# Transposes moved from TensorE to the DMA for the scan's gated outputs and the first feed-forward's products, with 48 adaLN pieces put off until the scan

## The chip, the cores and the metric

The kernel runs on one core of one Trainium2 chip. The metric is the device time in microseconds of one execution; of several runs the median counts. TensorE is called PE here, its weight load PEld, VectorE DVE, ScalarE ACT, GpSimd POOL and SyncE SP. SP does no arithmetic in this kernel: it issues the loads.

## The reference, cut to what matters

Two transformer layers over 256 tokens of width 2048, all in fp32. Layer 0 mixes by differential attention, layer 1 by a Mamba-2 scan; each is followed by a SwiGLU feed-forward. Both are modulated by a vector `c` (adaLN).

```python
c_act = silu(c)
for i in range(2):
    ada = c_act @ ada_w[i] + ada_b[i]                 # 2048 x 12288 weights a layer
    shift1, scale1, gate1, shift2, scale2, gate2 = split(ada, 6)
    h = rms_norm(x, norm1_g[i]) * (1 + scale1) + shift1
    m = diff_attention(h, ...) if i == 0 else mamba2_ssd(h, ...)
    x = x + gate1 * m
    h = rms_norm(x, norm2_g[i]) * (1 + scale2) + shift2
    g, u = split(h @ w_gate_up[i], 2)
    x = x + gate2 * ((silu(g) * u) @ w_down[i])

# mamba2_ssd, the part after the scan; 8 groups of 512 columns
y = y + d_skip * xs
y = y * silu(z)
y = rms_norm(y by group, norm_g)
return y @ w_out
```

Two places matter. `silu(g) * u` and the normalised `y` come out with tokens on the partitions, and the next matrix product needs them with features on the partitions: both are transposed in between.

## The kernel before, in words

**Tiles and units.** Every large weight is read in units of 256 rows by 512 columns (512 KB), each by one DMA on SP's queue into one of 7 `raw` buffers. `split_unit` makes two fp32r tiles of it: ACT casts `raw` to `wh` (line 287), DVE subtracts it to `wl`. PE then runs the three products wh*h, wl*h and wh*l of the two activation halves `ah` and `al`: 12 matmuls of 512 columns for a unit of 256 rows and all 256 tokens. `wh` and `wl` have 4 buffers each, so ACT and DVE work up to four units ahead of PE. Nearly all instructions are recorded under line 136, that of a metering helper, so the groups are told apart by tile names.

**Order.** The order on every engine is the order in which the program issues. `push_unit` puts the products of a unit into a queue `fifo`; `pop` runs them and then calls `tick`, which does the small work: it starts an adaLN piece when the accumulated `ada["rate"]` reaches one, uses the pieces loaded a tick earlier (`ripe`), and advances every active generator by one `yield` (`step_all`). A step of a generator is thus one unit of PE work.

**adaLN pieces.** The vectors of both layers are summed on DVE from 512 KB pieces of `ada_w`, which take `raw` buffers and SP's queue like the weights. `col_jobs` makes 32 pieces for one vector, used by `col_sum`: a multiply with a broadcast copy of `silu(c)` (`cB`, two tiles) and a sum along the row, on DVE, shown as CUSTOM_DVE_ANT_0. `ada_job` makes 34 pieces for a gate vector, used by a multiply-add into `acc`, and at each half POOL reduces `acc` over the partitions. In the first feed-forward 128 column pieces are queued (`m1` and `f1`, two vectors each) at a rate of 128/164 a unit; in the scan the 34 of gate `m1` at 34/140 (`ADA_UNITS`).

**First feed-forward (`ffn(0)`).** Eleven blocks `j`, each of 8 gate units and 8 up units. `up_done` multiplies silu(gate) by up into `sg` (DVE). A generator then makes `aT_j`: in layer 0 `rest`, with 8 PE transposes into `wk` banks and two ACT copies; in layer 1 `by_dma`, in which ACT writes the upper and lower 16-bit halves of `sg` apart into `halves`, the ACT queue issues a DMA transpose of 16-bit elements into `aT_j`, and `words` puts the halves together again (ACT) just before the split for the product with `w_down`.

**Scan.** Eight groups `g`, each of 8 units of `x` columns and 8 of `z` columns. `x_steps` is the convolution of a group, `y_steps` the scan and gating. At its end y is scaled by the norm (`r`), transposed by 4 PE transposes for each token block `b`, and DVE multiplies the result by the norm's gain into `yT`. `split(cp, g)` makes `ah` and `al` of it for the product with `ssd_w_out`; this begins at the last `z` block.

## Time and profile before

| | us |
|---|---|
| median of 3 runs | 2661.1 (2660.35 to 2661.39) |
| the profiled execution's own time | 2660.28 |
| its span in the trace | 2658.6 |
| first feed-forward, gate and up | 524 to 1005 |
| first feed-forward, down | 1010 to 1206 |
| scan, 8 groups | 1370 to 1741 |
| product with `ssd_w_out` | 1741 to 1920 |
| second feed-forward, gate and up | 1946 to 2424 |

The stage borders are read from the chain of waits and are rounded. Of an execution 1.7 us lie outside the span, and the profiled execution was 0.8 us faster than the median. In the rows `xN` is a count, "mean ns of one" includes what lies under the next instruction of the same engine, and "idle before" is idle time just before a group with what ended it.

### The profile page before, as it was taken

Reading aid. Unit: us, or ns where it says so; the run is one execution under the profiler, and the core shown is the slowest. Engines: PE = TensorE matmul, PEld = TensorE weight load, DVE = VectorE, ACT = ScalarE, POOL = GpSimd, SP = SyncE. Lnnn points to the kernel's source line nnn. Section 1 sums busy time; section 2 is a strip of 40 time slices with the busy share of each in tenths; the row PEclk is TensorE's granted clock in tenths of the full one; section 3 lists DMA queues with packets and bytes.
Section 4 is the critical chain, followed back from the end, with each engine's and each line's share of the span. In section 5 each row is a group of like instructions: output and inputs, shape, how many; then the busy total and the mean of one; then the engine's idle time right before and its main releaser. Section 6 shows DMA issues by size and latency. Waiting matters only on the chain.

```text
span 2658.6 us, 36556 instructions
## 1 busy us (share of the span) xinstructions
PE 2613.0 (98%) x13625; PEld 2186.6 (82%) x13625; DVE 1883.4 (71%) x2335; ACT 1361.5 (51%) x1897; POOL 200.7 (8%) x282
## 2 busy tenths in 40 slices
PE   7999999999999999999999999999999999999999
PEld 5777777788888888888999989988888888888887
DVE  3779887887788776777777787786654444446776
ACT  5445664644444444446546556565564444445554
POOL 5004331000000000001000010001000000000101
PEclk9999999999999999999999999999999999999999
DMA  9997888699999987885466566666756767677775
GB/s 335 336 350 282 328 297 323 228 343 330 341 341 339 333 320 260 284 291 176 168 229 227 207 245 224 207 225 201 223 158 206 208 203 208 204 207 235 292 282 188
DMA packets 211591, 690.34 MB, mean 260 GB/s; under 512 B 44962, under 2 KB 45299, under 8 KB 210003
## 3 DMA queue, kind: packets, MB, share of 16 engines
q1 hardware_dynamic: 186016, 678.59, 72.3%
q10 hardware_dynamic: 23954, 5.97, 2.2%
q0 software_dynamic: 1440, 3.44, 0.5%
q8 instruction: 107, 1.75, 0.3%
q14 instruction: 74, 0.60, 0.1%
HBM read 679.97 MB, written 2.16 MB: 257 GB/s over the span
## 4 chain that ended last, share of the span: by engine, by line
PE 88%; DVE 4%; DMA 3%; issue 2%; ACT 2%; POOL 0%; ACTq 0%; SPq 0%; DVEq 0%; POOLq 0%
PE mm L136 72%; PE wk L136 12%; PE po L136 4%; DVE wl L136 2%; DMA raw<-in_da_w_in 2%; DVE raw L136 1%; ACT wh L287 1%; DMA raw<-in_ada_m 1%; DMA piece<-in_ada_m 0%; DVE x L136 0%; DVE res L136 0%; ACT x L1042 0%; DMA stage<-in_ada_b 0%; DMA raw<-in_ssd_w_in 0%; DVE mx L136 0%
## 5 line engine op out<-in xcount | busy, mean ns | idle before, releaser
L287 ACT CAST wh<-raw 128x1024 fp32r<-128x1024 f32 (+1 forms) x888 | 925.7, 1046 | 1122.9 <-PE mm L136 715.1
L136 DVE TENSOR_TENSOR wl<-raw,wh 128x1024 fp32r<-128x1024 f32 (+1 forms) x888 | 1085.8, 1232 | 506.2 <-ACT wh L287 502.0
L136 PE MATMUL mm<-wh,ah 128*128 128x512 f32 (+1 forms) x2560 | 1012.8, 396 | 5.8 <-ACT wh L287 3.3
L136 PE MATMUL mm<-wl,ah 128*128 128x512 f32 (+1 forms) x2560 | 997.9, 390 | 1.0 <-DVE wl L136 1.0
L136 PE MATMUL mm<-wh,al 128*128 128x512 f32 (+1 forms) x2560 | 998.2, 390 | 0.0
L136 PEld LDWEIGHTS mm<-wh,ah 128*128 128x128 f32 x2560 | 481.6, 188 | 115.4 <-issue 12.1
L136 PEld LDWEIGHTS mm<-wh,al 128*128 128x128 f32 x2560 | 481.4, 188 | 101.8 <-DVE al L136 0.5
L136 PEld LDWEIGHTS mm<-wl,ah 128*128 128x128 f32 x2560 | 481.9, 188 | 99.5 <-DVE wl L136 2.8
L136 DVE CUSTOM_DVE_ANT_0 raw<-raw,cB,half 128x1024 f32<-128x1024 f32 x110 | 140.8, 1280 | 0.5
L136 DVE CUSTOM_DVE_ANT_0 raw<-raw,cB,bias 128x1024 f32<-128x1024 f32 x110 | 140.7, 1279 | 0.0
L136 PE MATMUL wk<-wh,ah 128*128 128x512 f32 x360 | 140.1, 389 | 0.0
L136 PE MATMUL wk<-wl,ah 128*128 128x512 f32 x360 | 140.1, 389 | 0.0
L136 PE MATMUL wk<-wh,al 128*128 128x512 f32 x360 | 140.1, 389 | 0.0
L531 POOL PARTITION_ALL_REDUCE gate<-acc x12 | 42.5, 3586 | 1273.9 <-DVE acc L136 1267.3
L136 PE MATMUL mm<-ah,wh 128*128 128x256 f32 x720 | 118.8, 285 | 0.0
L136 PE MATMUL mm<-ah,wl 128*128 128x256 f32 x720 | 117.7, 283 | 0.0
L136 PE MATMUL mm<-al,wh 128*128 128x256 f32 x720 | 117.7, 283 | 0.0
L136 DVE SCALAR_TENSOR_TENSOR acc<-raw,cT,acc 128x1024 f32<-128x1024 f32 x90 | 115.0, 1277 | 0.0
L136 PEld LDWEIGHTS mm<-ah,wh 128*128 128x128 f32 x720 | 100.2, 192 | 0.1
L136 PEld LDWEIGHTS mm<-ah,wl 128*128 128x128 f32 x720 | 100.2, 192 | 0.0
L136 PEld LDWEIGHTS mm<-al,wh 128*128 128x128 f32 x720 | 100.2, 192 | 0.0
L136 PEld LDWEIGHTS wk<-wh,al 128*128 128x128 f32 x360 | 67.6, 188 | 14.0
(317 smaller groups left out, 2095.7 us busy)
## 6 DMA issues: line engine op xcount, KB each, us to landing
raw<-in_ffn_w_gate_up SPq DMA_DIRECT2D x352, 512.0 KB, 4.7
raw<-in_ada_t SPq DMA_DIRECT2D x220, 512.0 KB, 5.4
raw<-in_ffn_w_down SPq DMA_DIRECT2D x176, 512.0 KB, 5.3
raw<-in_ssd_w_in SPq DMA_DIRECT2D x136, 512.0 KB, 4.6
raw<-in_da_w_in SPq DMA_DIRECT2D x96, 512.0 KB, 5.9
raw<-in_ada_w SPq DMA_DIRECT2D x96, 512.0 KB, 5.4
raw<-in_ssd_w_out SPq DMA_DIRECT2D x64, 512.0 KB, 4.5
raw<-in_ada_m SPq DMA_DIRECT2D x60, 512.0 KB, 6.0
```

The source lines that it names most:

```text
L136: return fn(dst, *a, **k)
L287: act.copy(wh[:, :, :n], raw)
L531: pool.partition_all_reduce(mods["G", key][:, o:o + 512], acc[:, i * 512:(i + 1) * 512], 128, ReduceOp.add)
```

## The change

In the first feed-forward `rest` goes and `by_dma` is used in both layers, with `words` after it: 88 PE transposes and 22 ACT copies go, 22 ACT copies to `halves`, 22 DMA transposes and 22 ACT copies to `word` come. In the scan the same is done for groups 0 to 6 with a tile `halves` of its own (group 7 keeps the PE transposes and uses that tile for its result): 56 PE transposes go. The two word copies wait `LANDING` steps (6, and 4 more for the second) after the second DMA transpose is issued, and DVE multiplies by the gain from `word` back into the planes. `split` first finishes the group's generator.

Of the 64 pieces of `f1` 16 stay in the first feed-forward (80 pieces there, so the rate is 80/164); 48 are put off to the scan, ahead of the 34 of the gate, at a rate of 82/156. Since `cB` shares its buffers with `acc`, `silu(c)` is kept in DRAM (`cd`, two DMAs of 4 KB) and read back as two broadcasts of 512 KB on SP when the scan stage is entered.

```diff
@@ -33,7 +33,8 @@
 RIPE = 1
 PACE = 4
 EPI = 3
-ADA_UNITS = 140
+ADA_UNITS = 156
+F1_EARLY = 16
 
 
 PIECES = {
@@ -47,6 +48,7 @@
 GRANULES = [(0, 256), (256, 256), (512, 512), (1024, 512), (1536, 512)]
 COLUMN_GRANULES = (1, 2, 3, 4)
 LAG = 2
+LANDING = 6
 
 
 class Laid:
@@ -1372,22 +1374,11 @@
                     yield
                 aT.append(t)
 
-            def rest():
-                yield
-                t = st["top" if j < 6 else "low"].tile([128, 4, 256], F32, name=f"aT_{j}")
-                for b in range(2):
-                    ps = bank("wk")
-                    for i in range(4):
-                        pe.transpose(ps[:, i * 128:(i + 1) * 128], sg[b][:, i * 128:(i + 1) * 128], ident)
-                    act.copy(t[:, :, b * 128:(b + 1) * 128], ps.rearrange("p (k t) -> p k t", k=4))
-                aT.append(t)
-            active.append(by_dma() if layer else rest())
+            active.append(by_dma())
 
         hl = {}
 
         def words(j, a):
-            if layer == 0:
-                return aT[j][:, 2 * a:2 * a + 2, :]
             w = st["low"].tile([128, 512], F32, tag="word", name="word", bufs=2)
             act.copy(w.bitcast(U16).rearrange("p (k t h) -> p h k t", k=2, h=2),
                      aT[j].rearrange("p (h k) t -> p h k t", h=2)[:, :, 2 * a:2 * a + 2, :])
@@ -1473,11 +1464,19 @@
         act.activation(H["aneg"], H["aneg"], AF.Exp)
         dve.tensor_scalar(H["aneg"], H["aneg"], -1.0, None, op0=ALU.mult)
 
+    later = deque()
+    cd = tc.dram_tile([1, 2048], F32, name="cd")
+
     def jobs0():
         col_jobs(1, 0, "m1")
         col_jobs(1, 1, "m1", n1c[1])
+        n = len(jobs)
         col_jobs(1, 3, "f1")
         col_jobs(1, 4, "f1", n2c[1])
+        while len(jobs) > n + F1_EARLY:
+            later.appendleft(jobs.pop())
+        for i in range(2):
+            sp.dma_start(cd[0:1, i * 1024:(i + 1) * 1024], cB[i][0:1, :])
 
     end = ffn(0, end, jobs0, False)
     if upto == "ffn0":
@@ -1489,6 +1488,13 @@
     S = {}
     norm = Norm(0, mods["S", "m1"], mods["T", "m1"])
     acd = tc.dram_tile([64, 256], F32, name="acd")
+
+    def later_jobs():
+        for i in range(2):
+            cB[i] = rowp.tile([128, 1024], F32, tag="acc", name="cB", bufs=2)
+            sp.dma_start(cB[i], bass.AP(tensor=cd.tensor, offset=cd.offset + i * 1024, ap=[[0, 128], [1, 1024]]))
+        jobs.extend(later)
+        later.clear()
 
     def enter():
         end["leave"]()
@@ -1508,6 +1514,7 @@
         pool.affine_select(out=tri, in_=tri, pattern=[[1, 128]], compare_op=ALU.is_ge, fill=0.0,
                            base=0, channel_multiplier=-1)
         S["bc"] = bp.tile([128, 16, 256], F32, name="bc")
+        later_jobs()
         ada_job(1, 2, fin_gate("m1"), gate=True)
         ada.update(rate=0.0)
 
@@ -1624,6 +1631,7 @@
         yield
         phb.close()
         S["y1"] = ph.enter_context(tc.tile_pool(name="y1", bufs=1))
+        S["halves"] = S["y1"].tile([128, 2, 512], F32, name="halves")
         S["gq"] = phq.enter_context(tc.tile_pool(name="gq", bufs=1, side="right"))
         load_decay(0)
         yield
@@ -1658,6 +1666,9 @@
         sp.dma_start(abc, bass.AP(tensor=acd.tensor, offset=acd.offset + 8 * g * 256,
                                   ap=[[0, 128], [256, 8], [1, 256]]))
 
+    def words(planes, b):
+        return planes[:, b].rearrange("p a t -> p (a t)").bitcast(F32).rearrange("p (k t) -> p k t", k=4)
+
     def y_steps(g, banks):
         h0 = 8 * g
         while ("abc", g) not in S:
@@ -1729,7 +1740,30 @@
         dve.tensor_scalar(y[0], y[0], r[0], None, op0=ALU.mult)
         yield
         r.append(rstd_of(ss[1], 1, 512, "yr"))
-        yT = S["yT", g] = S["y0" if g < 4 else "y1"].tile([128, 2, 4, 128], F32, name=f"yT{g}")
+        yp = S["y0" if g < 4 else "y1"]
+        if g < 7:
+            planes = S["yT", g] = yp.tile([128, 2, 8, 128], U16, name=f"yT{g}")
+            for b in range(2):
+                halves = S["halves"][:, b, :].bitcast(U16)
+                act.copy(halves.rearrange("p (h n) -> p h n", h=2),
+                         y[b].bitcast(U16).rearrange("p (n h) -> p h n", h=2))
+                if b:
+                    S["done", g] = True
+                yield
+                act.dma_start_transpose(planes[:, b], halves)
+                if b == 0:
+                    dve.tensor_scalar(y[1], y[1], r[1], None, op0=ALU.mult)
+                    yield
+            for b in range(2):
+                for _ in range(LANDING - 2 * b):
+                    yield
+                w = tmp("word")
+                act.copy(w.bitcast(U16).rearrange("p (k t h) -> p h k t", k=4, h=2),
+                         planes[:, b].rearrange("p (h k) t -> p h k t", h=2))
+                dve.tensor_tensor(words(planes, b), w.rearrange("p (k t) -> p k t", k=4),
+                                  H["cb"][:, 48 + 4 * g:52 + 4 * g, None].to_broadcast([128, 4, 128]), op=ALU.mult)
+            return
+        yT = S["yT", g] = S["halves"].rearrange("p b (k t) -> p b k t", k=4)
         for b in range(2):
             yield from take("wk")
             ps = bank("wk")
@@ -1776,7 +1810,9 @@
     def split(cp, g):
         if g == 7 and cp == 0:
             flush_steps()
-        hl[cp, g] = split_act([(lambda t, b=b: t[:, :, b * 128:(b + 1) * 128], S["yT", g][:, b]) for b in range(2)])
+        step_until(yg[g])
+        hl[cp, g] = split_act([(lambda t, b=b: t[:, :, b * 128:(b + 1) * 128],
+                                S["yT", g][:, b] if g == 7 else words(S["yT", g], b)) for b in range(2)])
 
     call(lambda: ada.update(rate=len(jobs) / ADA_UNITS))
     for g in range(8):
```

On PE, at the border between two blocks of the first feed-forward, before (`sg` is the product to be transposed, `ident` the identity; `mm` and `wk` are banks in PSUM):

```order
L136 MATMUL mm<-wl,ah 128x512
L136 MATMUL mm<-wh,al 128x512
L136 MATMUL wk<-ident,sg 128x128 x8
L136 MATMUL mm<-wh,ah 128x512
L136 MATMUL mm<-wl,ah 128x512
```

The row in the middle is gone after the change; the products on both sides follow each other. On ACT at the first such border, after the change (before, two copies of line 1382 from `wk` to `aT` stood here, and nothing else between the casts):

```order
L1358 ACTIVATE sg<-mm 128x512 x2
L289 CAST wh<-raw 128x1024 x9
L1370 COPY halves<-sg 128x1024
L289 CAST wh<-raw 128x1024
L1373 DMA_TRANSPOSE aT_5468<-halves 128x8x128
L289 CAST wh<-raw 128x1024
L1370 COPY halves<-sg 128x1024
L289 CAST wh<-raw 128x1024
L1373 DMA_TRANSPOSE aT_5468<-halves 128x8x128
L289 CAST wh<-raw 128x1024 x4
```

The two halves of the tokens go one after the other, one unit's cast between each step.

On DVE in the scan, in the first units of a `z` block, where the convolution of one group (`xc`) and the gating of the group before it (`xsd`) meet, before:

```order
L136 TENSOR_TENSOR xe<-xdt,toend 128x512
L136 TENSOR_TENSOR wl<-raw,wh 128x1024
L136 SCALAR_TENSOR_TENSOR xc<-mm,cw_5121,xc 128x253
L136 SCALAR_TENSOR_TENSOR xc<-mm,cw_5121,xc 128x254
L136 SCALAR_TENSOR_TENSOR xc<-mm,cw_5122,xc 128x255
L136 TENSOR_TENSOR xsd<-wk,xsd 128x512
L136 SCALAR_TENSOR_TENSOR xc<-mm,cw_5121,xc 128x253
L136 SCALAR_TENSOR_TENSOR xc<-mm,cw_5121,xc 128x254
L136 SCALAR_TENSOR_TENSOR xc<-mm,cw_5122,xc 128x255
L136 TENSOR_TENSOR wl<-raw,wh 128x1024
```

And after, from the third convolution tile of a group on (the ISA rows are `col_sum`; the short one reads out its sum):

```order
L138 SCALAR_TENSOR_TENSOR xc<-mm,cw_5125,xc 128x255
L138 TENSOR_TENSOR wl<-raw,wh 128x1024
L138 ISA raw,col4f_5139<-raw,cB,half 128x1024
L138 ISA col4f_5139 128x1
L138 TENSOR_TENSOR yT_13928<-word,cb 128x512
L138 TENSOR_TENSOR yi<-po,eac_10811 128x512
L138 TENSOR_TENSOR xsd<-xsd,yi 128x512
L138 SCALAR_TENSOR_TENSOR xc<-mm,cw_5124,xc 128x253
L138 SCALAR_TENSOR_TENSOR xc<-mm,cw_5124,xc 128x254
L138 SCALAR_TENSOR_TENSOR xc<-mm,cw_5125,xc 128x255
L138 TENSOR_TENSOR wl<-raw,wh 128x1024
```

A piece and the gain multiply of the group before (`yT<-word`) now stand between two subtractions of `wl` there.

## The prediction

> **What bounds the kernel now.** I read the page's first part, then the stages by windows, then the chain of waits in order of time, then the groups and timelines of the stages that the change touches.
>
> ```profile
> PE 2613.0 (98%) x13625; PEld 2186.6 (82%) x13625; DVE 1883.4 (71%) x2335; ACT 1361.5 (51%) x1897; POOL 200.7 (8%) x282
> ...
> core 0: us, PE busy (x) PEld busy (x) DVE busy (x) ACT busy (x) POOL busy (x), PEclk, DMA share, GB/s
> 524.00:1005.00 481.00, 481.00 (x2169) 399.30 (x2169) 382.21 (x467) 211.02 (x230) 2.16 (x4) 1.00 0.92 331
> 1369.75:1741.20 371.45, 371.09 (x2420) 336.38 (x2419) 291.31 (x357) 224.98 (x339) 21.17 (x28) 1.00 0.66 233
> 1946.00:2424.00 478.00, 478.00 (x2110) 395.92 (x2109) 232.07 (x210) 226.38 (x236) 0.00 (x0) 1.00 0.69 204
> ...
> 1485.10:1536.32 51.22, 51.22 (x339) 46.61 (x339) 40.22 (x49) 31.11 (x48) 2.24 (x5) 1.00 0.65 228
> ```
>
> PE is busy for the whole of both feed-forward stages and for all but 0.36 us of the scan; the last row is one group of the scan, which repeats every 51.22 us. A busy PE need not be a PE at its peak, so I look at what it runs. The chain in order of time (start, us, what):
>
> ```profile
> 782.87 43.54 PE mm L136 x192
> 827.28 43.54 PE mm L136 x192
> ...
> 1945.87 478.75 PE mm L136 x2112
> ```
>
> A block of the first feed-forward is 192 matmuls in 43.54 us, 0.2268 us each, and the next begins 44.41 us after it. The second feed-forward, whose transposes go by DMA already, runs 2112 matmuls in one piece at 478.75/2112 = 0.2267 us. So PE streams at the same pace in both, no wait is hidden in it, and what stands between two blocks (0.87 us) is the 8 transposes. The profile contains a full-length example of the changed feed-forward.
>
> **PE transposes removed: -15.7 us.** First feed-forward: 11 borders of 44.41 - 43.54 = 0.87 us, 9.6 us. Scan, PE's timeline around four of them:
>
> ```profile
> 1487.48 0.39 PE L136 MATMUL mm<-wh,al 128*128 128x512 f32 x1
> 1487.71 0.60 PE L136 MATMUL wk<-ident,xsd 128*128 128x128 f32 x4
> 1488.06 0.48 PE L136 MATMUL mm<-wh,ah 128*128 128x512 f32 x1
> 1488.38 0.39 PE L136 MATMUL mm<-wl,ah 128*128 128x512 f32 x1
> ```
>
> From the transposes' start to the next product's is 0.35 us, and that product takes 0.32 us to the one behind it in place of 0.23: 0.44 us for four. Two such sets for each of 7 groups make 6.2 us. As PE is the chain there, all 15.7 us come off unless something else falls behind. The rest of the sum is what that could be.
>
> **The added work and its prices**, by groups, DMA queues of three windows (540 to 980, 1390 to 1740 and 1960 to 2390 us) and one tile's landing times:
>
> ```profile
> L136 DVE CUSTOM_DVE_ANT_0 raw<-raw,cB,bias 128x1024 f32<-128x1024 f32 x110 | 140.7, 1279 | 0.0
> L136 DVE DVE_READ_ACCUMULATOR2_ANT half<- 128x1 f32 x110 | 8.9, 81 | 0.0
> L136 DVE SCALAR_TENSOR_TENSOR acc<-raw,cT,acc 128x1024 f32<-128x1024 f32 x90 | 115.0, 1277 | 0.0
> L1368 ACT COPY halves<-sg 128x1024 uint16<-128x1024 uint16 x22 | 22.9, 1043 | 0.0
> L1392 ACT COPY word<-aT 128x1024 uint16<-128x1024 uint16 x22 | 28.1, 1342 | 0.0
> ...
> q1 hardware_dynamic: 40703, 148.22, 93.0%
> ...
> q1 hardware_dynamic: 20665, 78.93, 64.2%
> ...
> q10 hardware_dynamic: 21120, 5.25, 12.2%
> ...
> aT<-halves ACTq DMA_TRANSPOSE x20, 5.5
> ...
> DMA to landing us min/median/max: 3.0/5.5/8.3
> ```
>
> A column piece costs DVE 1.28 + 0.08 = 1.36 us, a gate piece 1.28. A 512 KB load takes 0.930 x 440 us x 512 KB/148.22 MB = 1.45 us of all 16 DMA engines, a DMA transpose 0.122 x 430/20 = 2.62 us.
>
> First feed-forward. DVE loses 48 pieces, 65 us. ACT gains 22 x 1.04 us in a stage where it is busy 211 of 481; the 22 word copies come in the down product, where the second feed-forward has them too. DMA for a block: before 16 units and 16 x 128/164 = 12.5 pieces, 28.5 x 1.45 = 41.3 of 44.41 us (93%); after 16 + 7.8 loads and two transposes, 34.5 + 5.2 = 39.7 of 43.54 us (91%). No fuller than now, only burstier: 0 us. The cover is the seven raw buffers and the four units split ahead; without it the two transposes of a border would cost their 5.2 us.
>
> Scan, for a group (16 units). DVE: 40.22 us now, of which 16 x 34/140 = 3.9 gate pieces are 5.0; after, 16 x 82/156 = 8.4 column pieces are 11.4: 46.6 us of 51.22 - 0.87 = 50.35, or 93%. The gain multiply has the same size as now. ACT: 31.11 + 2 x (1.04 + 1.34) = 35.9 us, and two DMA issues. DMA: 0.642 x 51.22 + 4.5 x 1.45 + 2 x 2.62 = 44.6 us (89%). So DVE is the tightest, and its queue is in order; the units ahead of PE decide. Its idle time in that group, and the place where it is fullest:
>
> ```profile
> L136 DVE TENSOR_TENSOR wl<-raw,wh 128x1024 fp32r<-128x1024 f32 x16 | 19.4, 1218 | 3.9 <-ACT wh L287 3.9
> L136 DVE SCALAR_TENSOR_TENSOR xc<-mm,cw,xc 128x253 f32<-128x253 f32 (+2 forms) x12 | 5.8, 481 | 2.4 <-ACT xc L1520 2.0
> L136 DVE TENSOR_TENSOR abc<-abc,cb 128x1024 f32<-128x1024 f32 x2 | 2.4, 1220 | 1.1 <-ACT abc L1688 1.1
> L136 DVE TENSOR_TENSOR yT<-wk,cb 128x512 f32<-128x512 f32 x2 | 1.4, 688 | 1.3 <-PE wk L136 1.3
> L136 DVE TENSOR_TENSOR xsd<-wk,dsk 128x512 f32<-128x512 f32 x2 | 1.4, 685 | 1.9 <-PE wk L136 1.9
> ...
> 1526.15 1.22 DVE L136 TENSOR_TENSOR wl<-raw,wh 128x1024 fp32r<-128x1024 f32 x1
> 1530.48 1.21 DVE L136 TENSOR_TENSOR wl<-raw,wh 128x1024 fp32r<-128x1024 f32 x1
> ...
> 1536.08 0.48 PE L136 MATMUL mm<-wh,ah 128*128 128x512 f32 x1
> ```
>
> The cast for the unit that PE starts at 1536.08 follows the release of its buffer, so its `wl` is the one at 1530.48, done at 1531.7: 4.4 us early. After the change two pieces and a gain multiply come in front of it since DVE last stood caught up: 2 x 1.28 + 0.69 = 3.2 us, so about 1.2 us of lead is left. It should hold in most groups; where three pieces fall into the burst, PE waits some tenths. Lower bound 0; upper bound in the second rival. Near the lower one, since all waits but that for ACT's word copy are for work that a later DVE finds done: 1.5 us.
>
> A gain multiply waits for `word`, that for the landing. Six steps of 2.72 us are 16 us against 8.3 at most: 0 us, covered until the landing doubles. Behind the waiting copy on ACT the casts are queued, behind them `wl`.
>
> Last part: gate `m1` is now complete 16 units later, just where its residuals begin, and POOL's reductions slow DVE. The six and three subtractions under such reductions, and one reduction pair:
>
> ```profile
> 1205.62 11.12 DVE L136 TENSOR_TENSOR wl<-raw,wh 128x896 fp32r<-128x896 f32 x6
> ...
> 1802.86 4.93 DVE L136 TENSOR_TENSOR wl<-raw,wh 128x1024 fp32r<-128x1024 f32 x3
> ...
> 1798.38 7.06 POOL L531 PARTITION_ALL_REDUCE gate<-acc  x2 [6.60 <-issue]
> ```
>
> At 1.22 us for a subtraction they would be 7.3 and 3.7 us, so 1.3 to 3.8 us of DVE time are lost. The first two residuals need the gate's first half, which is reduced in the scan, so nothing waits for the 7.06 us; but two pieces (2.5 us) and the slowing come on top of four residual instructions, against some 6 us of lead (three units of 2.72 less a subtraction and the cast). 0.5 us, between 0 and 2.
>
> SP: two 4 KB writes and two 512 KB broadcasts. As loads the latter are 2 x 1.45 = 2.9 us of DMA at the entry of the scan stage, where the queue reads ahead; their buffers were released with the reduction above. 0 us, at most 2.9.
>
> **Sum.** -9.57 - 6.16 + 1.5 + 0.5 = -13.7 us. The span 2658.6 becomes 2644.9, with the 1.7 us around it 2646.6; the profiled execution lay 0.8 below the median of 2661.1, so 2647.4.
>
> **Rivals.**
> First, DVE falls behind a little in each group: a lead lost by 1 to 2 us in 5.7 groups (48 column pieces at 8.4 a group), 6 to 11 us in place of 1.5: 2652 to 2657. For it speaks the 93%, against it the lead above.
> Second, on the other side: DVE becomes the bound. Its waits for PE and ACT that are not for a cast come to 2.4 + 1.1 + 1.9 = 5.4 us a group; if they all stay, and each of two gain multiplies waits for its copy of 1.34 us, a group needs 46.6 + 5.4 + 2.7 = 54.7 us in place of 50.35. Over 5.7 groups that is +25 us: 2661.1 - 15.7 + 25 = 2670. It decides from a loss of 15.7/5.7 = 2.8 us a group. Against it: PE, DVE and ACT are coupled through four units, and a late DVE no longer waits for PE.
> Third, the DMA becomes the bound in the first feed-forward: if a transpose keeps the loads out for its whole 5.5 us to landing, a block needs 34.5 + 11 = 45.5 us, 1.1 us more than now, and 2661.1 + 12 - 6.2 = 2667. Against it: in the second feed-forward loads land between transposes and PE never stops, though at a DMA share of 0.69.
> The Trainium skill ("Advanced Engine Details and Errata", X-Bar Transpose) says that transposing DMAs are as fast as regular ones; this trace disagrees: 2.62 us for 256 KB against 1.45 us for 512 KB. By that page a transpose would be an estimated 0.72 us and this rival would vanish; the sum would stay the same.
> Fourth, the transposes' latency lands on the path: consumers read before the landing. 36 landings of 5.5 us would be 198 us, 2843; the unbroken 478.75 us speak against it. The Trainium skill ("VectorE: DVE Perf Modes", The three transpose paths and Rules for kernel authors) gives 390 ns on TensorE and 1309 ns by the DMA for a 128x128 block and advises TensorE where PSUM will do. That is a rule against this change, and it holds for the latency, as the 5.5 us agree; by the traces it is not what a PE-bound kernel pays.
> Fifth, nothing comes of it: the 0.87 us were slack that PE needs anyway for `wl`. Against it the equal pace of both feed-forwards; 2661.
>
> **How the numbers follow.** Forecast (2643.5 to 2651) 70%, first rival 13%, second 8%, third 4%, fourth 1%, fifth 4%. By these rows no more than 15.7 us can come off, which gives 2645.4; the low end 2643.5 adds the leeway of a run's spread and of waits not seen; the high end takes in the first rival, 2657. A measurement of this kernel tells about 0.2%, 5.3 us, from no change: faster is below 2655.8. That takes the forecast and nearly all of the first rival, less some doubt about how well a burst's lead is known: 80%. Same 10%, slower 10%.
>
> **What the profile after would show.** Right: blocks of the first feed-forward follow each other without a gap, 2112 matmuls in about 479 us; a scan group repeats every 50.4 us, with DVE near 46.6 us in it; DMA share near 0.9 in both. Wrong: PE idle before `mm` released by DVE `wl` in the scan (second rival: groups of 53 us or more), by ACT `wh` behind a DMA wait (third), or ACT waiting at a word copy for the planes (fourth).

## The result and the profile after

The changed kernel takes 2697.8 us (median of four runs, 2692.1 to 2708.4), the kernel before, beside it, 2661.2 us: ratio 1.0143, 95% interval 1.0128 to 1.0157. Medians and ratios leave out runs in a slower state; only one kernel below had such runs (2699.5 us, and 3235.3 us at a granted clock of 0.75). The change costs 36.6 us where 13.7 were to be gained. The profiled run is one of 2708.4 us (span 2706.7), 10.6 above the median, so its stages show the loss somewhat larger than the usual one. It is the longest of the four, which matters wherever a profile of an experiment is set beside it.

The page's first part, after:

```profile
PE 2618.5 (97%) x13480; PEld 2177.1 (80%) x13481; DVE 1881.1 (69%) x2335; ACT 1423.9 (53%) x1947; POOL 207.3 (8%) x282
```

PE has 145 matmuls fewer on record and is busy 5.5 us longer. Where the time lies is read from the stages. Windows of the kernel after: the first feed-forward's gate and up products, one group of the scan, and the whole of the SSD block from its first product to the second feed-forward's:

```profile
core 0: us, PE busy (x) PEld busy (x) DVE busy (x) ACT busy (x) POOL busy (x), PEclk, DMA share, GB/s
524.00:1005.00 481.00, 481.00 (x2124) 397.99 (x2124) 329.35 (x374) 230.85 (x240) 2.16 (x4) 1.00 0.95 292
1549.00:1609.50 60.50, 53.02 (x329) 47.71 (x329) 45.09 (x62) 34.96 (x52) 1.82 (x5) 0.95 0.86 238
1241.72:1981.67 739.95, 703.41 (x4216) 621.44 (x4215) 577.41 (x773) 432.26 (x631) 42.46 (x43) 0.98 0.76 236
```

The same stretch of the kernel before, between the same two instructions:

```profile
1246.81:1937.57 690.76, 690.03 (x4271) 619.12 (x4271) 517.59 (x676) 405.40 (x603) 34.00 (x43) 1.00 0.62 211
```

The SSD block took 690.8 us and takes 740.0: the whole loss and more. PE, which stood still for 0.7 us in it, stands 36.5 us. It is also busy 13.4 us longer, though 6.2 us of transposes are gone: the granted clock falls from 1.00 to 0.98, 0.95 in the group shown. At 0.98 the clock takes some 15 us (0.02 x 740); the other 5 of these 19.6 us are not explained. A group takes 60 us in place of 51.2, and DVE works 45 us in it. That is less than the 46.6 us forecast, so DVE's work is not what fills the group.

Ahead of the block the kernel gains 5.1 us (1241.72 against 1246.81), behind it loses 4.0. The chain of waits in the first feed-forward, after:

```profile
520.54 207.05 PE mm L138 x912
727.84 265.97 PE mm L138 x1174
...
1006.38 14.29 DMA raw<-in_ffn_w_down
```

The blocks follow each other without a gap, as forecast; a load that takes 14.29 us then stops the chain at the border to the down product.

How the DMA fares in the scan, after: the landing times of `halves` (the transposes), then of `raw` (the loads) from 1430 to 1790 us, and last of the loads of the kernel before, from 1390 to 1740 us:

```profile
DMA to landing us min/median/max: 3.8/12.8/21.0
...
DMA to landing us min/median/max: 3.3/5.6/18.9
...
DMA to landing us min/median/max: 3.1/4.6/8.9
```

And the transposes' queue from 1430 to 1790 us (packets, MB, share of 16 engines):

```profile
q10 hardware_dynamic: 13728, 3.41, 9.9%
```

13 transposes hold the engines for 0.099 x 360/13 = 2.74 us each, as priced (2.62). But they land in 12.8 and up to 21 us, not in 5.5 and at most 8.3, and some loads now land in up to 18.9 us, where none took more than 8.9. One group shows what that does. The chain there:

```profile
1557.23 18.60 DMA raw<-in_ssd_w_in
```

And the timelines of ACT, DVE and PE (in brackets the idle time before the row and what ended it):

```profile
1575.93 1.04 ACT L289 CAST wh<-raw 128x1024 fp32r<-128x1024 f32 x1 [8.87 <-DMA raw<-in_ssd_w_in]
...
1577.01 1.22 DVE L138 TENSOR_TENSOR wl<-raw,wh 128x1024 fp32r<-128x1024 f32 x1 [9.87 <-ACT wh L289]
...
1573.06 0.64 PE L138 MATMUL mm<-ah,wl 128*128 128x256 f32 x4
1577.03 1.22 PE L138 MATMUL mm<-ah,wh 128*128 128x256 f32 x4 [3.33 <-ACT wh L289]
1578.05 1.05 PE L138 MATMUL mm<-al,wh 128*128 128x256 f32 x4
...
1606.87 0.66 PE L138 MATMUL wk<-ident,xc 128*128 128x128 f32 x4 [4.15 <-ACT xc L1537]
```

The two transposes of the group are issued at 1550.6 and 1556.1. A load issued at 1557.23 takes 18.6 us. ACT, in order, stands 8.87 us at its cast, DVE 9.87 us behind ACT, and then PE 3.33. DVE has lost 10 us of work, and the stretch where convolution and gating meet comes next: 30 us later PE still waits 4.15 us for the convolution. After the gap four matmuls take 1.05 us in place of 0.64: the clock is at 0.67 from 1576 to 1579 (0.50 from 1577.03 to 1580.44). PE's waits in the scan, from 1430 to 1780 us:

```profile
PE wk L138 <- ACT xc L1537: 17.2, 5, 4.2
PE mm L138 <- DVE wl L138: 6.6, 4, 2.0
PE mm L138 <- ACT wh L289: 5.3, 3, 3.3
```

Most of it is not the late load itself but the convolution behind DVE's backlog. What starts the backlog is the late load: the chain of waits from 1430 to 1780 us runs through four loads of 14.9 to 18.6 us, 67 us in all, each issued within 4 us after the second of a pair of transposes.

### The profile page after: what moved, and what is told of

It reads as the page before. It is cut to its first block, busy times and chain, and to the rows that moved or that the text cites. A ratio compares the mean times of both kernels' runs of the same rounds, so it can differ in the third digit from the quotient of the medians.

```text
span 2706.7 us, 36323 instructions
## 1 busy us (share of the span) xinstructions
PE 2618.5 (97%) x13480; PEld 2177.1 (80%) x13481; DVE 1881.1 (69%) x2335; ACT 1423.9 (53%) x1947; POOL 207.3 (8%) x282
## 4 chain that ended last, share of the span: by engine, by line
PE 72%; DVE 10%; DMA 8%; ACT 5%; issue 4%; POOL 1%; SPq 0%; ACTq 0%; DVEq 0%; POOLq 0%
PE mm L138 59%; PE wk L138 9%; DVE wl L138 4%; PE po L138 4%; DMA raw<-in_ssd_w_in 3%; DMA raw<-in_da_w_in 2%; ACT wh L289 1%; DVE xc L138 1%; DMA raw<-in_ffn_w_down 1%; DVE raw L138 1%; DMA raw<-in_ada_t 1%; DMA raw<-in_da_w_out 1%; DVE acc L138 1%; ACT word L1383 1%; DVE xsd L138 1%
## 5 line engine op out<-in xcount | busy, mean ns | idle before, releaser
L138 DVE TENSOR_TENSOR al<-word,ah 128x512 fp32r<-128x512 f32 x44 | 28.5, 688 | 91.9 <-ACT ah L394 91.9
```

The costliest lines, as they stand in the source:

```text
L138: return fn(dst, *a, **k)
```

## The experiments

Each ratio is to runs of the kernel before that were taken beside the experiment; their medians lie between 2658.7 and 2660.0 us.

Theory A: transposes in flight beside dense loads make each other late, and the scan, whose DVE was forecast to be over 90% busy, can't make up for it. Theory B: the 48 moved pieces alone make DVE the bound (the prediction's second rival). Theory D, a form of A: two transposes in flight at once are what makes the loads late.

**The parts one by one.** Each kernel has some parts of the change and not the others. The move:

```diff
-ADA_UNITS = 140
+ADA_UNITS = 156
+F1_EARLY = 16
...
+        later_jobs()
```

> The kernel before with only the 48 pieces moved from the first feed-forward to the scan; all transposes stay on PE. Theory A (DMA transposes in flight beside dense loads slow each other, and the scan, its DVE over 90% busy, cannot make up for the late loads): without transposes there is little to lose, scan groups of 51.2 to 52.5 us against about 60 in the changed kernel, 2661 to 2670 us in all. Theory B (the moved pieces alone make DVE the bound of the scan, the second rival of the prediction): groups of 56 us or more, 2685 to 2710 us. Raw loads in the scan land in 3 / 5 / 9 us (least, median, most) by A as by B.

2663.7 us, ratio 1.0015 (1.0005 to 1.0024). Windows of the scan, 1430 to 1780 us, of the kernel before, of the changed one and of this one (columns as in the windows above):

```profile
1430.00:1780.00 350.00, 350.00 (x2242) 315.66 (x2241) 277.03 (x336) 215.90 (x329) 21.24 (x28) 1.00 0.65 227
1430.00:1780.00 350.00, 319.81 (x1988) 283.30 (x1987) 271.82 (x359) 210.76 (x311) 17.94 (x24) 0.97 0.86 247
1430.00:1780.00 350.00, 350.00 (x2237) 315.20 (x2237) 311.98 (x401) 214.06 (x327) 27.82 (x30) 1.00 0.77 271
```

Landing of this kernel's loads there:

```profile
DMA to landing us min/median/max: 3.1/5.0/6.6
```

PE never stops with DVE busy 312 of 350 us, where the changed kernel's PE is busy 319.8 in the same window. Theory B is out: the moved work alone costs the scan nothing. The SSD block is 5.3 us longer all the same; 3.4 of them are PE's only wait of the out stage (1780 to 1930 us), for subtractions behind the late gate:

```profile
PE wk L137 <- DVE wl L137: 3.4, 2, 2.5
```

The scan's transposes alone:

```diff
+            planes = S["yT", g] = yp.tile([128, 2, 8, 128], U16, name=f"yT{g}")
...
+                act.dma_start_transpose(planes[:, b], halves)
```

> The kernel before with only the scan's 14 sets of transposes by DMA; no piece moved, first feed-forward as before. PE saves 6.2 us. Theory A: the transposes land in 8 to 20 us here too, though the load on the DMA is lower (38 of 50.35 us a group), ACT stands several us at a late raw, but DVE (about 40 of 51 us busy) catches up before the dense stretch: groups of 51 to 54 us, 2660 to 2678 us. Theory B (DVE's work alone): groups of 50.4 us, 2655 us. If the landings stay at 3 to 8 us with this lighter load, it is the load on the DMA that matters and not the transposes by themselves.

2662.7 us, 1.0013 (1.0000 to 1.0027). The same window:

```profile
1430.00:1780.00 350.00, 338.68 (x2138) 302.74 (x2137) 268.13 (x325) 239.75 (x353) 29.13 (x28) 1.00 0.81 233
```

Landing there, of the transposes and then of the loads:

```profile
DMA to landing us min/median/max: 4.0/14.0/20.6
...
DMA to landing us min/median/max: 3.1/5.9/17.2
```

Transposes and loads are about as late as in the changed kernel (16.1 us median of the transposes over the same 350 us), with the DMA at 0.81 and DVE busy 77% of the time; PE stands 11.3 us, in a profile of one of the longer runs (2670.0 us). So the lateness is the transposes', not the moved pieces'. With slack on DVE it costs some 9 us by the medians (6.2 saved, and still 2.8 slower), not the 39 that the scan's transposes cost in the changed kernel (33 more than with the scan on PE, below, and the 6.2 saved).

The first feed-forward's transposes alone, then both kinds without the move:

```diff
-            active.append(by_dma() if layer else rest())
+            active.append(by_dma())
```

> The kernel before with only the first feed-forward's 22 transposes by DMA; no piece moved, the scan as before. PE saves 9.6 us. By the prices of the prediction a block then needs 28.5 x 1.45 + 5.2 = 46.5 us of the DMA engines, against 43.5 of PE: the DMA would be the bound, +2.1 us a block against now, 2685 us. Theory A adds slow landings, loads late by up to 19 us: 2685 to 2700 us, with PE gaps in the feed-forward. Theory B says nothing of this stage: 2651.5 us.

2714.3 us, 1.0194 (1.0176 to 1.0211). PE is busy 424.55 of the 461 us from 524 to 985, at a DMA share of 1.00. The sum that said 46.5 us of DMA a block was right in kind: without the move that stage is DMA-bound. In size it was not: it gave 24 us more than before, where 54 were measured, and theory A's 2700 us were exceeded too. The chain of waits shows one part that the sum did not have: from 520 to 1010 us 18.2% of it are landings of transposes, up to 21.1 us long, which SP's queue waits for before it issues the next load (109 us in 11 waits from 524 to 1005 us).

> The changed kernel without the move of the 48 pieces: both kinds of transposes by DMA. If the parts add up, its time less the one before is the sum of the differences of the two kernels with one kind each. Theory A: the scan alone costs little (0 to +17 us), the first feed-forward is DMA-bound (+20 to +40): 2680 to 2715 us. Theory B: scan 50.4 us a group and no loss there: 2645 us where the first feed-forward keeps pace.

2721.6 us, 1.0225 (1.0186 to 1.0264), near the sum of the two differences (54.3 + 2.8 against 61.6) and 6 us above the forecast.

The scan back on PE (the branch `if g < 7` and `words` taken out of the changed kernel's scan):

```diff
-        if g < 7:
-            planes = S["yT", g] = yp.tile([128, 2, 8, 128], U16, name=f"yT{g}")
...
+        yT = S["yT", g] = S["y0" if g < 4 else "y1"].tile([128, 2, 4, 128], F32, name=f"yT{g}")
```

> The changed kernel with only the scan's transposes back on PE; the first feed-forward's by DMA and the 48 pieces moved as in it. From the kernel with the move alone (+3.7 us against before, scan groups of 51.2 us) it differs by 11 borders of 0.87 us that PE no longer works. Theory A (transposes and moved pieces do harm only where they meet in the scan): first feed-forward 481 us to the same marker without gaps, scan as before: 2661 + 3.7 - 9.6 + 3 us for the late loads at the border to the down product = 2658 us, 2652 to 2661. If it is over 2670 us, the first feed-forward's transposes cost more than the changed kernel's trace showed, and the loss is not the scan's alone.

2664.9 us, 1.0019 (1.0010 to 1.0029). The scan's window:

```profile
1430.00:1780.00 350.00, 350.00 (x2237) 315.07 (x2236) 312.07 (x402) 214.48 (x329) 27.63 (x29) 1.00 0.78 271
```

33 us of the loss are gone with the 14 DMA transposes. The time is above the 2658 expected: the first feed-forward loses 2.9 us beside late loads in its profile (258.10 busy of 261 us from 724 to 985), and its transposes bring no gain over the move alone.

**Which load matters.** The changed kernel with the moved pieces' sums cut, and with their loads cut:

```diff
+        n = 128 if moved else 1024
-        dve.tensor_tensor_reduce(rv, rv, cB[hf], 1.0,
+        dve.tensor_tensor_reduce(rv[:, :n], rv[:, :n], cB[hf][:, :n], 1.0,
```

> The changed kernel, but each of the 48 moved pieces is summed over 128 of its 1024 columns (so their sums are incomplete); all loads stay. DVE loses some 0.9 us x 8.4 pieces = 8 us a scan group, the DMA keeps its 89%. Theory A in the form that late loads leave DVE a backlog that it can't work off: groups of 51 to 54 us, 2655 to 2675 us, with the landings as slow as in the changed kernel (13 us median). If the DMA itself (its load, or SP's queue) sets the pace, the groups stay at 57 us or more and the time at 2685 to 2700 us. Theory B: as the first, with PE waits gone.

2682.1 us, 1.0092 (1.0063 to 1.0121). The scan's window:

```profile
1430.00:1780.00 350.00, 335.71 (x2101) 298.78 (x2100) 264.22 (x381) 230.45 (x343) 27.66 (x28) 0.99 0.90 267
```

```diff
-                sp.dma_start(rv, col_item(layer, vec, kt, hf))
+                if moved:
+                    item = bass.AP(tensor=ada_t.tensor, offset=item.offset, ap=[[1024, 128], [1, 128]])
+                sp.dma_start(rv[:, :128] if moved else rv, item)
```

> The changed kernel, but each of the 48 moved pieces loads 128 of its 1024 columns (64 KB in place of 512 KB), and its sum runs over 1024 columns of what is in the chip (so these sums are wrong); DVE's work is as in the changed kernel. The DMA loses 7/8 x 8.4 x 1.45 = 10.7 us a group. If the DMA's load sets the pace: groups of 51 to 53 us, landings of 5 to 10 us, 2650 to 2670 us. If DVE's backlog after one late load does: landings about as slow as in the kernel with the scan alone by DMA (14 us median at a light load), groups of 54 to 59 us, 2675 to 2695 us.

2674.5 us, 1.0060 (1.0039 to 1.0082). The scan's window:

```profile
1430.00:1780.00 350.00, 336.89 (x2124) 301.51 (x2122) 297.41 (x381) 233.53 (x345) 27.74 (x27) 0.99 0.81 228
```

Landing of the transposes there:

```profile
DMA to landing us min/median/max: 4.0/11.0/16.3
```

The cuts take PE's idle time from 30.2 to 14.3 and 13.1 us; neither brings it to zero, and the transposes still land in 11 to 12 us (16.1 in the changed kernel over the same 350 us). By the medians the short sums give back 15.7 and the short loads 23.3 of the 36.6 us. So DVE's slack and the DMA's slack each hold off about half of the loss. "DVE's backlog alone" and "the DMA's load alone" both miss.

**How many, and how close.** One of the two transposes of a group back on PE:

```diff
+                    break
+            yield from take("wk")
+            ps = bank("wk")
+            for i in range(4):
+                pe.transpose(ps[:, i * 128:(i + 1) * 128], y[1][:, i * 128:(i + 1) * 128], ident)
```

> The changed kernel with one of the two transposes of each scan group back on PE (the second half of the tokens); 7 DMA transposes in the scan in place of 14, one in flight at a time. If two transposes in flight at once are what makes them slow: landings of 5 to 8 us, groups of 51.5 to 53 us, about 2660 us. If each costs its share: landings of 8 to 14 us, groups of about 55 us and 2675 to 2683 us, half of the loss. If one late load is enough: groups of 58 us or more, 2690 us.

2666.0 us, 1.0022 (1.0009 to 1.0035). The scan's window:

```profile
1430.00:1780.00 350.00, 346.45 (x2205) 311.34 (x2204) 311.81 (x398) 225.66 (x339) 33.02 (x28) 1.00 0.87 275
```

Landing there, of the transposes and then of the loads:

```profile
DMA to landing us min/median/max: 5.9/10.7/12.1
...
DMA to landing us min/median/max: 3.4/5.2/13.3
```

Half of the transposes, an eighth of the idle time: not in proportion to their number. This profile is of one of the shorter runs (2658.75 us; they go from 2658.2 to 2672.2), but the medians say the same: one transpose a group costs 1.1 us against the scan on PE (2664.9), two cost 33. The landings did not come down to the 5 to 8 us expected if two in flight were the whole cause. Both by DMA, but further apart, five units more by the edit and 20 to 24 us in the trace, where the changed kernel has 5.4:

```diff
-                yield
+                for _ in range(1 + 5 * b):
+                    yield
                 act.dma_start_transpose(planes[:, b], halves)
```

> The changed kernel with the two transposes of a scan group six units (about 16 us) apart instead of two, so that the first has landed before the second is issued; everything else, their number too, as in the changed kernel. Theory D (it is two transposes in flight at once that make a load beside them late by 13 to 19 us, and that lateness starts the loss): landings of 6 to 12 us as with one half by DMA, loads at most 13 us, groups of 51.5 to 54 us, 2660 to 2675 us. Against it, theory of the dose (14 transposes in the scan take that much of the DMA and of DVE's slack wherever they stand): groups of 57 us or more, 2685 to 2700 us.

2674.1 us, 1.0059 (1.0036 to 1.0081). The scan's window:

```profile
1430.00:1780.00 350.00, 342.41 (x2150) 305.94 (x2149) 303.84 (x391) 238.78 (x353) 25.23 (x28) 0.99 0.92 276
```

Landing there, of the transposes and then of the loads:

```profile
DMA to landing us min/median/max: 4.9/8.2/14.5
...
DMA to landing us min/median/max: 3.4/5.5/15.2
```

The same work and as many DMAs, 24 us less by the medians; PE's idle time falls from 30.2 to 7.6 us, in a profile of the shortest of four runs. This is what theory D says, for most of the scan's loss. It is not all of it: a single transpose still makes loads land in 13 to 15 us. And the edit moves something else too: the gain multiplies come later with it and no longer stand between the convolution's instructions on DVE (at 1590.41 and 1601.14 us, the convolution from 1575.77 to 1589.4; in the changed kernel one is at 1600.94 in the midst of it). They take 0.69 us each; what their place is worth was not tried apart.

**The late gate, and the first feed-forward.** With the scan on PE, the moved pieces queued behind the gate `m1` (the copies of `silu(c)` are read back behind the gate too, which with six empty entries ahead of it makes the queue 89 long and the rate 89/156):

```diff
+        ada_job(1, 2, fin_gate("m1"), gate=True)
         later_jobs()
-        ada_job(1, 2, fin_gate("m1"), gate=True)
```

> The kernel with the scan on PE (first feed-forward by DMA, 48 pieces moved), but the moved pieces are queued behind the 34 pieces of the gate m1, so that this gate is complete halfway through the scan and not under the first residuals of the output product. Theory of the gate: all kernels with the move have 3.4 us of PE idle between 1780 and 1930 us, where the kernel before has none; it comes from the late reductions and goes with them: no idle there, 3 us less than with the scan on PE: about 2661.5 us by the medians (2664.9 there), 2657 to 2663. If the 3.4 us stay, they have another cause, and the time stays at 2665.

2657.7 us, 0.9999 (0.9984 to 1.0014). PE's waits from 1780 to 1930 us:

```profile
PE wk L137 <- DVE wl L137: 0.7, 1, 0.7
PE wk L137 <- DVE xn L137: 0.4, 1, 0.4
```

Of the 3.4 us 2.3 are gone; the other 5 us to the kernel with the scan on PE are not explained by the gate. About 1 us of them is that the kernel before was as much faster beside this run (2658.7 against 2659.7). In this profile PE did not stop in the first feed-forward, where it did there, but it is of one of the shorter runs (2653.4, of 2650.4 to 2668.2). This is the best version found, and it is no faster than the kernel before.

Then the first feed-forward's two transposes further apart, and one of the two on PE:

```diff
-                    yield
+                    for _ in range(1 + 6 * b * (layer == 0)):
+                        yield
                     act.dma_start_transpose(t[:, :, b * 128:(b + 1) * 128], halves)
```

> As the kernel with the gate first, and the two transposes of each block of the first feed-forward six units further apart. Theory D says that it is two transposes in flight that let loads land 13 to 15 us late there too, with 1.7 to 4.8 us of PE idle in that stage in four profiles: landings of 6 to 11 us, no idle, another 2 to 5 us off: 2656 to 2659 us. If the lateness is that of one transposes beside dense loads (DMA 91% busy), nothing changes: within 1.5 us of the kernel with the gate first.

2662.9 us, 1.0030 (1.0005 to 1.0055), runs from 2657.0 to 2687.3. The profile, of one of 2680.2 us, has in the stage (524 to 985 us):

```profile
524.00:985.00 461.00, 444.40 (x1922) 362.68 (x1921) 298.58 (x346) 203.12 (x212) 2.16 (x4) 0.99 0.98 278
```

The transposes land no sooner (13.7 us median, from 524 to 1005 us; 7.0 in the profile of the gate first, 13.0 in the changed kernel), ACT waits 170.5 us in all for loads, where the kernel with the gate first has 42.3, and PE stands 16.6 us. As this is a longer run and that was a shorter one, the difference is not all the edit's. But the 2 to 5 us that theory D promised do not come: it finds no support in the first feed-forward, where the DMA is 0.95 and more busy. Why the distance helps in the scan and not there is open.

```diff
+                    if layer == 0 and b == 1:
...
+                            pe.transpose(ps[:, i * 128:(i + 1) * 128], sg[1][:, i * 128:(i + 1) * 128], ident)
```

> The kernel with the gate first (scan on PE, 48 pieces moved), with one of the two transposes of each block of the first feed-forward back on PE. PE saves 11 x 0.44 = 4.8 us there in place of 9.6. If the first feed-forward loses its 5 us or so (in three of six profiles with both by DMA) because it has two transposes beside a DMA that is 91% busy, it loses nothing now: DMA 34.5 + 2.6 = 37.1 of 44 us (84%), no PE idle, loads at most 12 us, 2655 to 2659 us, with less spread than the 2650 to 2668 of the gate first. If single transposes start it as well, PE idle of 1 to 5 us stays and the time is 2659 to 2664 us.

2660.9 us, 1.0002 (0.9993 to 1.0011), spread 2657.5 to 2665.3. PE never stops in the stage, loads land in at most 13.5 us, and the 4.8 us saved don't show in the median, which is above the 2655 to 2659 expected: inconclusive within the uncertainty. The profiled run is one of the longer ones (2665.0), so its length does not come from this stage.

**Dense loads where the prediction had looked.** The kernel before with 80 extra loads in the second feed-forward, which nothing reads; then the same with all transposes on PE:

```diff
+            if layer == 1:
+                def more(i):
...
+                    sp.dma_start(rv, col_item(1, 1, i % 16, i // 16 % 2))
+                jobs.extend([lambda i=i: more(i) for i in range(80)])
```

> The kernel before, with 80 more loads of 512 KB in the second feed-forward's gate and up products, 7.8 a block as the changed kernel has them in the first; nothing reads what they load, so DVE and ACT do nothing for them. The DMA has 16 + 7.8 loads and two transposes a block: 34.5 + 5.2 = 39.7 of 43.5 us (91%) in place of 0.66. Theory A (dense loads are what makes the transposes slow): landings rise from 3.0 / 5.5 / 8.3 us to about 5 / 12 / 21, loads of up to 15 us appear, PE stands 0 to 10 us in the stage: 2661 to 2675 us. If landings stay at 5.5 us, the slowness in the first feed-forward and in the scan comes from something else there (DVE, the waits of ACT, other code).

2676.9 us, 1.0069 (1.0044 to 1.0093), just above the forecast, runs from 2663.0 to 2693.0; the profile caught one of 2663.0, with PE never idle. Gate and up products of the second feed-forward in two parts:

```profile
1950.00:2210.00 260.00, 260.00 (x1149) 215.29 (x1148) 128.13 (x117) 121.82 (x130) 0.00 (x0) 1.00 0.88 297
2210.00:2440.00 230.00, 230.00 (x1017) 190.44 (x1016) 113.93 (x102) 110.33 (x113) 0.00 (x0) 1.00 0.87 283
```

> The same 80 extra loads, but the second feed-forward's transposes on PE as well: 23.8 loads a block, 34.5 of 44.4 us (78%), no DMA transposes anywhere. PE works 11 x 0.87 = 9.6 us more. Theory A: no load over 9 us, no PE idle, 2661 + 9.6 = 2671 us. If loads of 13 us and more and PE idle appear here too, the extra loads are the cause by themselves and not their meeting with transposes.

2669.2 us, 1.0032 (1.0020 to 1.0044), runs from 2666.4 to 2670.4, as 11 x 0.87 us more on PE say; no load lands later than 7.6 us and PE is never idle. So the extra loads alone cost nothing and vary by 4 us (five runs); with the transposes they vary by 30 (eight runs).

> The kernel with 80 more loads in the second feed-forward again, for a second profile: its runs went from 2663 to 2693 us, and the one profiled was a 2663 with PE never idle. If the spread comes from transposes that land late beside the loads, a profile of a longer run (2673 us and more) shows in that stage landings of 15 to 21 us, loads of 14 us and more, and PE idle there that adds up to the difference, with nothing changed elsewhere. If the difference lies in other stages, the spread is not the transposes'.

> The same kernel a third time, with the same expectation: the longer the run, the more PE idle in the second feed-forward's gate and up products, 0 to 30 us.

2662.9 and 2683.6 us. The longer one, the same two parts, and the waits there:

```profile
1950.00:2210.00 260.00, 255.04 (x1111) 209.17 (x1110) 120.53 (x107) 113.38 (x119) 0.00 (x0) 0.99 0.87 275
2210.00:2440.00 230.00, 220.18 (x946) 179.07 (x946) 104.53 (x92) 101.08 (x105) 0.00 (x0) 0.99 0.90 282
```

```profile
ACT wh L287 <- DMA raw<-in_ffn_w_gate_up: 132.2, 87, 6.6
PE mm L136 <- ACT wh L287: 8.9, 5, 2.9
PE mm L136 <- DVE wl L136: 5.7, 8, 0.8
```

And of the first of the three profiles (2663.0 us):

```profile
ACT wh L287 <- DMA raw<-in_ffn_w_gate_up: 21.0, 15, 5.2
```

The longer run loses its time there. It enters the stage 3.7 us ahead of that short one (1936.6 against 1940.4 us); then PE stands 14.8 us where it stood not at all, and its matmuls are slower (475.2/2057 = 0.231 us against 490/2166 = 0.226, at a clock of 0.99), some 10 us more. The other short run (2662.9) has 2.3 us of PE idle. DVE is busy half of this stage and no moved piece is summed. So transposes beside dense loads stall PE by themselves; from run to run they do so more or less. Landings of 6.2 to 7.8 us median (at most 16.1) are less than the 12 expected, so the DMA's mean share (0.88 here, 0.81 in the scan with its landings of 14 us) does not alone set them.

## Why the prediction was wrong

What held: 0.87 us a border of PE's work (blocks without gaps, 207.05/912 = 0.227 us a matmul), the engine time of a transpose (2.74 against 2.62), and DVE's work in a group (45 against 46.6). The move, whose gain the prediction did not price apart, is needed beside the first feed-forward's transposes (without it the kernel is 61.6 us slower, in place of 36.6).

The step that failed is the DMA's part of the scan, "DMA: 0.642 x 51.22 + 4.5 x 1.45 + 2 x 2.62 = 44.6 us (89%). So DVE is the tightest", with its companion in the first feed-forward, "No fuller than now, only burstier: 0 us". Both count a transpose on the DMA as 2.62 us of throughput, and no step has a price for what it does to the loads beside it. In the scan the late ones among these land in 13 to 19 us, where none took more than 8.9 before. Seven raw buffers and four units do not cover that: ACT stands, DVE behind it, and the convolution comes late. The scan's term, 1.5 us, came out at 49.2 + 6.2 - 3.4 = 52 us in the profile (the block's loss, the PE work saved in it, the gate's part).

The transposes' own landing was mis-sized as well: it was taken from the second feed-forward, where the DMA is 0.69 busy, as 5.5 and at most 8.3 us, and is 12.8 and at most 21.0 in the scan. But the wait that the prediction tied to it ("Six steps of 2.72 us are 16 us against 8.3 at most: 0 us, covered until the landing doubles") did not come: in the whole SSD block ACT never waits for the planes before a word copy. With groups of 60 us, six steps had become some 22 us (60/16 x 6). So that 0 us held, and the landing that mattered was the loads'. PE's largest wait, 17.2 us for the convolution, is none of the signs that the prediction named for being wrong; of those, the waits for `wl` (6.6 us) and for `wh` behind a load (5.3 us) came.

The second rival named the right place and sign (DVE behind in the scan, groups of 54.7 us; they took 60), but not the cause: the work alone costs the scan nothing, it only takes away the slack with which a late load would be made good. The third rival had the cause, a transpose that keeps loads out, and the wrong place: it argued from a block's sum in the first feed-forward, where DVE has slack (329 of 481 us).

The first feed-forward's term, -9.57, came out at 4.2 us in the profile: from its first block to the SSD block 721.2 us, against 725.4 before. PE stands 3.2 us around the late load at the border to the down product (71.78 us busy of 75 from 985 to 1060).

Three smaller terms. The gate `m1`: 0.5 us forecast, 0 to 2; 3.4 measured, of which 2.3 go with the order. The word copies in the down product were given no price: in the kernel with the gate first PE waits 0.8 us for subtractions at its end, where the kernel before and that with the move alone have none; that the copies make it is not shown. The first feed-forward, from its first block to the SSD block, took 716.9 us in that profile against 725.4 before, a gain of 8.4 of the 9.6. And the range: every case within it took the transposes' landing from the same row and left the loads' as it was, so nothing in it allowed for that not to hold.

## What to carry over

A DMA that shares the engines with a dense stream of loads has two prices: its engine time, and what it adds to the landing of the loads beside it. The second can't be read from a stage where the DMA is two thirds busy; read it, or measure it, at the density of the place where the DMA will go. Where an in-order engine feeds the bound one with little slack, a few late loads cost more than the work saved, and moving other work there takes away exactly the slack that would have absorbed them.

## What had not been expected of the hardware

Two DMA transposes in flight beside loads let single 512 KB loads land in up to 18.9 us where they took at most 8.9 before, while the DMA reads as busy (in the group shown a share of 0.99 to 1.44 from 1555 to 1573 us, at 167 to 236 GB/s; the share adds up the packets' own times, so it can exceed 1). The packets show part of the why. From 1546 to 1552 us the loads' queue moves 1.95 MB in 532 packets, with 95.3% of the 16 engines' time, 0.17 us a packet. From 1558 to 1564, with the transposes' packets among them, it moves 1.06 MB in 287 packets with 86.2%, 0.29 us a packet, and 1.06 MB again in the next 6 us. So for 12 us the loads go at little more than half their rate, and those issued then queue up. Why a load's packet takes longer there is open, as is why the same program then differs by 30 us from run to run. The Trainium skill ("DMA: Bandwidth & Descriptors", Issuing engines are not separate DMA queues) says that DMAs of all queues run on the same 16 engines and interleave. The trace agrees, as far as it goes: from 1558 to 1564 us 605 packets of the transposes' queue start among the 287 of the loads'. An argument from it, which no run shows: a transpose has 13728/13 = 1056 packets, 66 an engine; if each stands behind one 4 KB packet of a load (1.45 us/8 = 0.18 us) and takes 2.74/66 = 0.04 us itself, it lands after some 14.5 us, about the landings measured. The lateness of the loads does not follow from it.

After a gap of 3.33 us the granted clock of PE is 0.50 for 3.41 us (from 1577.03 to 1580.44), so a wait costs more than its length: in the SSD block PE is busy 13.4 us longer for less work. The Trainium skill ("TensorE: Matmul & The Clock Gate", Part 1: The HAM clock gate) has the clock halved after an idle window of about 3.4 us. The trace agrees on the halving, but shorter gaps were enough here: with one of 2.50 us that ends at 1893.95 (the clock is 0.50 from 1894.5 to 1897.8) and one of 2.95 us that ends at 1485.39 (0.50 from 1485.0 to 1488.3).

SP's loads came to wait for the transposes too. Of its queue's waits in the scan, after, the largest of this kind (before, none of them is for a DMA):

```profile
SPq L285 <- DMA yT<-halves: 27.3, 5, 9.2
```

A load that waits so for an earlier transpose has no data to do with it. In the group shown it was not what ended last: the load that stopped ACT had been issued before, and the chain of the scan from 1430 to 1780 us has no landing of a transpose. In the kernel with the first feed-forward's transposes alone such waits do lie on the chain. How much of the loss they make was not tried apart.
